# Recurrent block of a hybrid decoder trunk: where the high half of the gated product is rounded, when its last low half is formed, and the order of the last output projections

## The chip, the cores and the metric

The kernel runs on one core of a Trainium2 chip. The metric is device time in microseconds (us) of one execution; lower is better. The kernel computes a two-layer decoder trunk on 256 tokens of width 1024. All its large matrix products are done with split operands: each fp32 number is held as a high part (rounded to the matmul format fp32r) and a low part (the rest), and each product of two 128-row tiles is three matmuls, high x high, high x low and low x high.

## The reference, cut to what matters

```
h = x                                      # (1, 256, 1024)
for l in range(2):
    hn = rms_norm(h, mix_norm_g[l])
    mix = even_mixer(...) if l == 0 else odd_mixer(hn, ...)
    h = h + mix
    h = h + conv_ffn(rms_norm(h, ffn_norm_g[l]), ...)
return rms_norm(h, final_norm_g)

def odd_mixer(x, w_in, conv_w, conv_b, w_a, b_a, w_x, b_x, lam, w_out):
    gate_branch, xr = split(x @ w_in, 2)
    xr = causal_dwconv(xr, conv_w, conv_b)
    r, i = sigmoid(block_gemm(xr, w_a) + b_a), sigmoid(block_gemm(xr, w_x) + b_x)
    log_a = -8 * r * softplus(-lam)
    h = linear_scan(exp(log_a), sqrt(1 - exp(2 * log_a)) * i * xr)
    y = h * gelu(gate_branch)              # the gated product
    return y @ w_out                       # the output projection
```

The even mixer (attention and gated linear attention) also ends in a product with a 1024 x 1024 matrix, and the same helper computes it.

## The kernel before, in words

Everything is kept transposed: 128 channels on the partitions, 256 tokens along the free axis. A weight matrix comes in chunks of 128 x 1024 fp32 (512 KB). `load_w` keeps a short queue of chunks; `issue_w` starts the transfer of chunk i on SyncE, then forms its high part on ScalarE (`wh`, line 134) and its low part on VectorE (`wl`, line 135). Those two are called weight splits here. There are 204 chunks. Chunk 104 (`L1_C0`) is the first of layer 1's mixer; by the order in `L1_ORDER` its chunks 124 to 127 (`L1_C0 + 20` to `+ 23`) are the four chunks of the first half of the output projection ("o"), and 128 to 131 are the four of the second half ("h"); 132 is the first of the feed-forward network that follows.

The recurrent block handles channels in four pairs of 128-channel tiles, n = 0 to 3. For pair n, `recur` (line 690) makes the recurrence `hh[n]` with a scan on VectorE, and `finish` (line 697) makes the gated product. `finish` has one GeLU on ScalarE and three VectorE instructions on 128 x 512 elements: line 700 multiplies `hh` by `gb` straight into the rounded high part `Y[.., 0, :]`, line 701 makes the same product in fp32 in place, and line 702 subtracts the first from the second to give the low part `Y[.., 1, :]`. In the trace the tile `Y` is named `r`; the mixer result of layer 0 is named `m`.

`out_proj` (line 216) computes the output projection. Its eight 128 x 256 results m = 0 to 7 share four PSUM banks `acc[0]` to `acc[3]`, two to a bank (j = 0 and 1). `part(q, c)` adds k-tiles 2q and 2q+1 for four of the results; the four parts need only pairs 0 and 1 of the gated product, and each has 24 matmuls. `tail(n, fin)` then adds k-tiles 4 to 7 for the two results of bank n, again 24 matmuls, and calls `fin` for each result as soon as it is complete. K-tiles 4 and 5 come from pair 2, k-tiles 6 and 7 from pair 3. In `tail` all twelve matmuls of j = 0 come first, then `fin` of j = 0, then the twelve of j = 1. `fin` is `residual` (line 210): VectorE adds the result to the residual stream (line 211), ScalarE squares it for the next norm (line 172), VectorE accumulates the squares (line 179), and the two engines form the next product's input (lines 205 and 206).

The order of instructions on each engine is not the order of the program text: the framework schedules the whole program with a timing model of its own and then fixes one order for each engine. Engines then run their orders and wait for each other on semaphores. `order(first, then)` adds an edge that puts `then` behind `first` in that order, without a semaphore when both are on one engine. `state["hooks"]` holds such edges for weight splits: an entry under `("l", i)` puts the low weight split of chunk i on VectorE behind the given instruction. `passes` (line 141) issues the three matmuls for each k-tile in its list and returns them.

Of the kernel before, what the change touches and what calls it, by code (L numbers as in the profile page):

```python
# [8 lines left out]
F32 = mybir.dt.float32  # L9
# [3 lines left out]
AF = mybir.ActivationFunctionType  # L13
# [17 lines left out]
L1_C0 = 104  # L31
# [31 lines left out]
def trunk(ctx: ExitStack, tc: tile.TileContext, xT, w, wgk, wgk2, vec, cst, mskf, out):  # L63
    nc = tc.nc
# [7 lines left out]
    def bank(name, tag="g"):  # L72
        return pp.tile([P, 512], F32, tag=tag, bufs=BANKS[tag], name=name)

    def order(first, then):
        tc.add_manual_dep(then.ins, first.ins.name,
                          mybir.DependencyInfo(mybir.DependencyClass.NoSync, mybir.DependencyReason.DATA),
                          reason="issue order")
# [7 lines left out]
    def V(name, i):  # L86
        o = VOFF[name] + i
        return vt[:, o:o + 1]
# [25 lines left out]
    state = {"hooks": {}, "i": 0, "q": []}  # L114
# [3 lines left out]
    def load_w():  # L118
        while len(state["q"]) <= LOOK and state["i"] < NCH:
            state["q"].append(issue_w())  # L120
        return state["q"].pop(0)
# [19 lines left out]
    def passes(ps, ops, first=True, last=True, skip=False):  # L141
        n = len(ops)
        out = []
        for i, (ah, al, bh, bl) in enumerate(ops):
            for j, (a, b) in enumerate(((ah, bh), (ah, bl), (al, bh))):
                out.append(nc.tensor.matmul(ps, a, b, start=first and i + j == 0, stop=last and i == n - 1 and j == 2,  # L146
                                            skip_group_check=skip))
        return out

    def gemm(ps, wc, X, k0=0, first=True, last=True, nk=KT, skip=False):  # L150
        return passes(ps, [(wc[0][:, k * P:(k + 1) * P], wc[1][:, k * P:(k + 1) * P], X[:, k0 + k, 0, :], X[:, k0 + k, 1, :])
                    for k in range(nk)], first, last, skip)
# [8 lines left out]
    def new_m(name):  # L161
        return xp.tile([P, KT, 2, S], F32R, tag="m", name=name)
# [53 lines left out]
    def out_proj(M):  # L216
        acc = [bank(f"psout{i}", "g" if i < 3 else "l") for i in range(4)]
        opened = {}

        def part(q, c):  # L220
            wh, wl = load_w()
            for m in range(4 * c, 4 * c + 4):
                ps = acc[m // 2][:, (m % 2) * S:(m % 2 + 1) * S]
                ops = []
                for k in range(2):
                    o = k * 512 + (m % 4) * P
                    ops.append((wh[:, o:o + P], wl[:, o:o + P], M[:, 2 * q + k, 0, :], M[:, 2 * q + k, 1, :]))
                first = m not in opened
                mms = passes(ps, ops, first and m % 2 == 0, False, skip=True)
                if first:  # L230
                    opened[m] = mms[0]
                    if m % 2:
                        order(opened[m - 1], mms[0])

        def tail(n, fin):
            wh, wl = load_w()
            for j in range(2):
                ps = acc[n][:, j * S:(j + 1) * S]
                ops = []
                for k in range(4):  # L240
                    o = k * S + j * P
                    ops.append((wh[:, o:o + P], wl[:, o:o + P], M[:, 4 + k, 0, :], M[:, 4 + k, 1, :]))
                passes(ps, ops, False, True, skip=True)
                fin(ps, 2 * n + j)
        return part, tail

    def out_fin(X, gname, gi, norm):
        return lambda ps, m: residual(ps, m, X, gname, gi, norm)
# [29 lines left out]
    with tc.tile_pool(name="l0", bufs=1) as lp, tc.tile_pool(name="l0r", bufs=4) as lr:  # L278
# [106 lines left out]
        ps = bank("psbq")  # L385
# [9 lines left out]
        ps = bank("psbk")  # L395
# [81 lines left out]
        for nm in ("q", "k"):  # L477
            for m in range(2):
                ps = bank("psa")
# [56 lines left out]
        for pr in range(4):  # L536
            for j in range(2):
                PT[2 * pr + j] = softmax(2 * pr + j)
            ps = bank("pso", "t")
# [15 lines left out]
        for pr in range(4):  # L555
            ps = bank("pob", "l")
# [14 lines left out]
        for m in range(4):  # L571
            ps = bank("psog")
# [26 lines left out]
        fin = out_fin(X, "ffn_g", 0, norm)  # L599
# [40 lines left out]
    with tc.tile_pool(name="l1", bufs=1) as lp, tc.tile_pool(name="l1r", bufs=3) as lr:  # L640
        def pairs(name, dt=F32):
            return [lp.tile([P, 2, S], dt, name=f"{name}{n}") for n in range(4)]

        xc, rr, ii, aa, uu, tt, hh, gb = [pairs(n) for n in ("xc", "rr", "ii", "aa", "uu", "tt", "hh", "gb")]
        C1 = [lp.tile([P, 2, 2, S], F32R, name=f"c1{n}") for n in range(4)]
        Y = new_m("r")
        def xr_pair(n):
            ps = bank("psx")
            for j in range(2):
                gemm(ps[:, j * S:(j + 1) * S], load_w(), X)  # L650
            v = lr.tile([P, 2, S], F32, tag="v", name="v")
            nc.vector.tensor_mul(v, ps.rearrange("p (j t) -> p j t", j=2), rs[:, None, :].to_broadcast([P, 2, S]))
            for j in range(2):
                m = 2 * n + j
                nc.scalar.activation(xc[n][:, j, :], v[:, j, :], AF.Identity, bias=V("rc_b", m), scale=V("rc_w", 24 + m))
                for d in (1, 2, 3):
                    nc.vector.scalar_tensor_tensor(xc[n][:, j, d:], v[:, j, 0:S - d], V("rc_w", (3 - d) * 8 + m),
                                                   xc[n][:, j, d:], op0=ALU.mult, op1=ALU.add)
            split(C1[n][:, :, 0, :], C1[n][:, :, 1, :], xc[n])

        def gb_pair(n):
            ps = bank("psgb")
            for j in range(2):
                gemm(ps[:, j * S:(j + 1) * S], load_w(), X)
            nc.vector.tensor_mul(gb[n], ps.rearrange("p (j t) -> p j t", j=2), rs[:, None, :].to_broadcast([P, 2, S]))

        def gates(n):
            wh, wl = load_w()
            for gi, (dst, bn) in enumerate(((rr, "b_a"), (ii, "b_x"))):
                ps = bank("psgt", "s")  # L670
                for mt in range(2):
                    ops = []
                    for k in range(2):
                        o = gi * 512 + k * 256 + mt * 128
                        ops.append((wh[:, o:o + P], wl[:, o:o + P], C1[n][:, k, 0, :], C1[n][:, k, 1, :]))
                    passes(ps[:, mt * S:(mt + 1) * S], ops)
                for mt in range(2):
                    act(SIG, dst[n][:, mt, :], ps[:, mt * S:(mt + 1) * S], AF.Sigmoid,
                                         bias=V(bn, 2 * n + mt))
            nc.vector.tensor_mul(ii[n], ii[n], xc[n])  # L680

        def decay(n):
            for j in range(2):
                m = 2 * n + j
                nc.vector.tensor_scalar(rr[n][:, j, :], rr[n][:, j, :], cc[:, m:m + 1], None, op0=ALU.mult)
            for dst, f, sc in ((tt, AF.Tanh, 1.0), (uu, AF.Exp, 2.0), (aa, AF.Exp, 1.0)):
                act(EXP, dst[n], rr[n], f, scale=sc)
            nc.vector.scalar_tensor_tensor(tt[n], uu[n], 1.0, tt[n], op0=ALU.add, op1=ALU.mult)

        def recur(n):  # L690
            act(SQRT, tt[n], tt[n], AF.Sqrt, scale=-1.0)
            nc.vector.tensor_mul(uu[n], tt[n], ii[n])
            nc.gpsimd.memset(aa[n][:, :, 0:1], 0.0)
            fl = lambda t_: t_.rearrange("p a b -> p (a b)")
            nc.vector.tensor_tensor_scan(fl(hh[n]), fl(aa[n]), fl(uu[n]), 0.0, op0=ALU.mult, op1=ALU.add)

        def finish(n):
            s2 = slice(2 * n, 2 * n + 2)
            act(GELU, gb[n], gb[n], AF.Gelu_apprx_tanh)
            nc.vector.tensor_mul(Y[:, s2, 0, :], hh[n], gb[n])  # L700
            nc.vector.tensor_mul(hh[n], hh[n], gb[n])
            nc.vector.tensor_sub(Y[:, s2, 1, :], hh[n], Y[:, s2, 0, :].bitcast(F32))  # L702

        part = norm1 = None
        X1 = X
        for tok in L1_ORDER.split():
            if tok[0] == "o":
                if part is None:
                    part, tail = out_proj(Y)
                part(int(tok[1]), int(tok[2]))  # L710
            elif tok[0] == "h":
                if norm1 is None:
                    use(SQRT)
                    norm1 = Norm()
                    X1 = new_x()
                tail(int(tok[1]), out_fin(X1, "ffn_g", 1, norm1))
            else:
                {"x": xr_pair, "b": gb_pair, "g": gates, "e": decay, "s": recur, "f": finish}[tok[0]](int(tok[1:]))
# [112 lines left out]
```

## Time and profile before

| | |
|---|---|
| time, median of 3 runs | 649.29 us (645.31 to 649.8) |
| the profiled execution's own time | 646.74 us |
| its span | 645.0 us |
| TensorE matmuls busy | 630.7 us, 98% of the span |
| VectorE busy | 513.3 us, 80% |
| ScalarE busy | 406.0 us, 63% |
| mean granted TensorE clock | 0.993 of full speed |

The profile is one execution. Its span is the time from the first to the last instruction, and 1.74 us lie around it. Times in the rows are counted from the start of the span. In the timeline views each row is a run of like instructions on one engine: start, duration, engine, line, operation, output and inputs by name, count, and in square brackets the idle time before the first, with what ended it. A matmul's row is longer than the step to the next, because matmuls overlap.

### The profile page before, as it was taken

The numbers are of one execution on the slowest core, as the hardware profiler recorded it, in microseconds if no ns is written. First come the engines' busy times: TensorE is split into PE (matmuls) and PEld (weight loads), VectorE is DVE, ScalarE is ACT, GpSimd is POOL, SyncE is SP. The second block draws the span as 40 slices with busy tenths as digits, with TensorE's granted clock in tenths as the row PEclk, the third lists the DMA queues.
The fourth block names the chain that finished last, engine by engine and source line by source line (L and its number), as shares of the span: only waits on it lengthen the run. The fifth ranks groups of instructions, "written<-read, shape, count | busy, mean of one in ns | idle before, by whom it ended". The sixth has DMA issues, their size and how long they took to land.

```text
span 645.0 us, 12988 instructions
## 1 busy us (share of the span) xinstructions
PE 630.7 (98%) x5218; PEld 613.1 (95%) x5218; DVE 513.3 (80%) x902; ACT 406.0 (63%) x662; POOL 8.9 (1%) x36
## 2 busy tenths in 40 slices
PE   7999999999999999999999999989999999999995
PEld 4998888899999999999999999989999999999995
DVE  6699985467999999996577859996999999986532
ACT  7798454646776666675476578966666667674310
POOL 5000000000000000000000000000000000000000
PEclk8999999999999999999999999999999999999998
DMA  8823511534264485555277505544466545455201
GB/s 303 312 100 131 196 67 66 197 132 164 74 239 173 184 313 194 195 177 183 102 282 269 201 2 196 196 154 151 155 229 229 196 163 193 179 210 204 99 1 66
DMA packets 31516, 110.90 MB, mean 172 GB/s; under 512 B 3648, under 2 KB 4192, under 8 KB 31456
## 3 DMA queue, kind: packets, MB, share of 16 engines
q1 hardware_dynamic: 31456, 110.07, 47.5%
q8 instruction: 41, 0.67, 0.4%
q14 instruction: 19, 0.16, 0.1%
HBM read 109.01 MB, written 1.05 MB: 171 GB/s over the span
## 4 chain that ended last, share of the span: by engine, by line
PE 93%; DVE 2%; ACT 2%; issue 1%; DMA 1%; SPq 0%; DVEq 0%; ACTq 0%
PE psu L146 42%; PE psd L146 21%; PE psout L146 5%; PE psx L146 4%; PE psa L146 4%; PE pst L146 3%; PE psgb L146 3%; PE pl L465 2%; PE psog L146 2%; PE psgt L146 2%; PE psbq L146 1%; DVE wl L135 1%; PE psbk L146 1%; PE pss L514 1%; DMA big<-xT 1%
## 5 line engine op out<-in xcount | busy, mean ns | idle before, releaser
L134 ACT ACTIVATE wh<-w 128x1024 fp32r<-128x1024 f32 x204 | 212.5, 1056 | 112.8 <-PE psu L146 71.8
L135 DVE TENSOR_TENSOR wl<-w,wh 128x1024 fp32r<-128x1024 f32 x204 | 246.9, 1219 | 39.6 <-ACT wh L134 38.7
L146 PE MATMUL psu<-x,wh 128*128 128x256 f32 x1536 | 270.5, 280 | 0.0
L146 PEld LDWEIGHTS psu<-x,wh 128*128 128x128 f32 x1536 | 234.6, 189 | 0.0
L146 PE MATMUL psu<-x,wl 128*128 128x256 f32 x768 | 214.3, 280 | 0.0
L146 PEld LDWEIGHTS psu<-x,wl 128*128 128x128 f32 x768 | 144.7, 189 | 0.0
L146 PE MATMUL psd<-y,wh 128*128 128x256 f32 x768 | 134.6, 280 | 0.0
L146 PEld LDWEIGHTS psd<-y,wh 128*128 128x128 f32 x768 | 116.9, 188 | 0.0
L146 PE MATMUL psd<-y,wl 128*128 128x256 f32 x384 | 106.7, 279 | 0.0
L619 DVE SCALAR_TENSOR_TENSOR c<-v,big,c 128x255 f32<-128x255 f32 (+1 forms) x192 | 83.6, 475 | 0.0
L146 PEld LDWEIGHTS psd<-y,wl 128*128 128x128 f32 x384 | 72.1, 188 | 0.0
L617 ACT ACTIVATE c<-v,big 128x256 f32<-128x256 f32 x96 | 51.7, 589 | 0.6 <-DVE v L612 0.6
L172 ACT ACTIVATE sq<-big 128x256 f32<-128x256 f32 x40 | 15.4, 407 | 50.7 <-DVE big L211 50.6
L211 DVE TENSOR_TENSOR big<-big,psd 128x256 f32<-128x256 f32 x16 | 6.7, 420 | 35.3 <-PE psd L146 35.3
L612 DVE TENSOR_TENSOR v<-psu,rs 128x512 f32<-128x512 f32 x48 | 32.5, 681 | 0.0
L146 PE MATMUL psout<-r,wh 128*128 128x256 f32 x128 | 23.1, 282 | 2.0 <-DVE r L702 2.0
L146 PE MATMUL pst<-wh,x 128*128 128x256 f32 x128 | 24.2, 285 | 0.0
L146 PE MATMUL psout<-m,wh 128*128 128x256 f32 x128 | 23.7, 285 | 0.0
L146 PE MATMUL psx<-x,wh 128*128 128x256 f32 x128 | 23.0, 281 | 0.0
L146 PE MATMUL psgb<-x,wh 128*128 128x256 f32 x128 | 22.7, 280 | 0.0
L146 PE MATMUL psa<-x,wh 128*128 128x256 f32 x128 | 22.5, 280 | 0.0
L99 ACT ACT_TABLE_LOAD x17 | 21.8, 1283 | 1.0 <-PEq L823 0.7
(202 smaller groups left out, 850.5 us busy)
## 6 DMA issues: line engine op xcount, KB each, us to landing
w<-w SPq DMA_DIRECT2D x204, 512.0 KB, 4.3
big<-xT SPq DMA_DIRECT2D x4, 256.0 KB, 3.8
out<-o SPq DMA_DIRECT2D x4, 256.0 KB, 2.4
ct<-cst SPq DMA_DIRECT2D x1, 384.0 KB, 8.0
big<-vec SPq DMA_DIRECT2D x1, 224.0 KB, 7.9
mf<-mskf SPq DMA_DIRECT2D x1, 192.0 KB, 8.0
wg<-wgk SPq DMA_DIRECT2D x1, 64.0 KB, 2.0
big<-cst SPq DMA_DIRECT2D x1, 64.0 KB, 5.2
```

The source lines that it names most:

```text
L99: ld = nc.scalar.preload_act_table_set(name)
L134: hi = nc.scalar.activation(wh, wt, AF.Copy)
L135: lo = nc.vector.tensor_sub(wl, wt, wh.bitcast(F32))
L146: out.append(nc.tensor.matmul(ps, a, b, start=first and i + j == 0, stop=last and i == n - 1 and j == 2, skip_group_check=skip))
L172: ins = nc.scalar.activation(sq, t, AF.Square)
L211: nc.vector.tensor_add(h[:, m, :], h[:, m, :], ps)
L465: nc.tensor.matmul(pv[:, :, :, cs], Kb[li, I][:, ts_], qv[:, :, :, cs], start=True, stop=True)
L514: nc.tensor.matmul(ps[:, 128:384], q[r, P:S], k[r, 0:S], start=True, stop=False)
L612: nc.vector.tensor_mul(v, ps.rearrange("p (j t) -> p j t", j=2), rs[:, None, :].to_broadcast([P, 2, S]))
L617: nc.scalar.activation(c[:, j, :], v[:, j, :], AF.Identity, bias=V("fc_b", layer * 48 + ch), scale=wv(2))
L619: nc.vector.scalar_tensor_tensor(c[:, j, d:], v[:, j, 0:S - d], wv(2 - d), c[:, j, d:], op0=ALU.mult, op1=ALU.add)
```

## The change

In `finish`, the high part is no longer a second multiplication on VectorE. The fp32 product is formed first (VectorE), ScalarE copies it with rounding into the high part, and VectorE then subtracts as before. The low part of the last pair, n = 3, is put ahead of the low weight split of chunk `L1_C0 + 25` (129, the second chunk of the second half of the projection). In `tail`, the 24 matmuls go by pairs of k-tiles: k-tiles 4 and 5 for j = 0, the same for j = 1, then k-tiles 6 and 7 for j = 0, then for j = 1, and these 24 are kept in that order. `tail` is called by both layers, `finish` by layer 1 alone.

```
         def tail(n, fin):
             wh, wl = load_w()
-            for j in range(2):
+            mms = []
+            for kp, j in ((0, 0), (0, 1), (1, 0), (1, 1)):
                 ps = acc[n][:, j * S:(j + 1) * S]
                 ops = []
-                for k in range(4):
+                for k in (2 * kp, 2 * kp + 1):
                     o = k * S + j * P
                     ops.append((wh[:, o:o + P], wl[:, o:o + P], M[:, 4 + k, 0, :], M[:, 4 + k, 1, :]))
-                passes(ps, ops, False, True, skip=True)
-                fin(ps, 2 * n + j)
+                mms += passes(ps, ops, False, kp == 1, skip=True)
+                if kp:
+                    fin(ps, 2 * n + j)
+            for a_, b_ in zip(mms, mms[1:]):
+                order(a_, b_)
         return part, tail
...
         def finish(n):
             s2 = slice(2 * n, 2 * n + 2)
             act(GELU, gb[n], gb[n], AF.Gelu_apprx_tanh)
-            nc.vector.tensor_mul(Y[:, s2, 0, :], hh[n], gb[n])
             nc.vector.tensor_mul(hh[n], hh[n], gb[n])
-            nc.vector.tensor_sub(Y[:, s2, 1, :], hh[n], Y[:, s2, 0, :].bitcast(F32))
+            nc.scalar.activation(Y[:, s2, 0, :], hh[n], AF.Copy)
+            lo = nc.vector.tensor_sub(Y[:, s2, 1, :], hh[n], Y[:, s2, 0, :].bitcast(F32))
+            if n == 3:
+                state["hooks"].setdefault(("l", L1_C0 + 25), []).append(lo)
```

## Rows read from the trace of the kernel before

**Rows 1.** The page, busy time by engine: us (share), instructions.
```profile
PE 630.7 (98%) x5218; PEld 613.1 (95%) x5218; DVE 513.3 (80%) x902; ACT 406.0 (63%) x662; POOL 8.9 (1%) x36
```

**Rows 2.** The longest wait of TensorE's matmuls, whole span: us in total, times, longest.
```profile
PE psout L146 <- DVE r L702: 2.0, 2, 1.5
```

**Rows 3.** Timeline of TensorE around the second half of layer 1's output projection.
```profile
418.59 0.63 PE L146 MATMUL psout<-r,wh 128*128 128x256 f32 x4
419.68 0.38 PE L146 MATMUL psout<-r,wh 128*128 128x256 f32 x1 [0.47 <-DVE r L702]
...
422.48 0.27 PE L146 MATMUL psout<-r,wh 128*128 128x256 f32 x1
424.29 0.39 PE L146 MATMUL psout<-r,wh 128*128 128x256 f32 x1 [1.54 <-DVE r L702]
...
432.41 0.40 PE L146 MATMUL psu<-x,wh 128*128 128x256 f32 x2
```

**Rows 4.** Projection matmuls (psout) by stretch: length; PE, PEld, DVE busy (count); clock, DMA.
```profile
419.60:424.00 4.40, 3.07 (x24) 2.87 (x24) 0.00 (x0) 1.00 0.38 133
424.00:434.00 10.00, 8.28 (x68) 8.07 (x68) 3.34 (x8) 1.00 0.44 153
```

**Rows 5.** Timeline of VectorE in layer 1's block, to the residual adds.
```profile
406.53 0.68 DVE L702 TENSOR_TENSOR r<-hh,r 128x512 fp32r<-128x512 f32 x1
...
411.43 1.23 DVE L135 TENSOR_TENSOR wl<-w,wh 128x1024 fp32r<-128x1024 f32 x1 [0.67 <-ACT wh L134]
...
416.02 0.68 DVE L700 TENSOR_TENSOR r<-hh,gb 128x512 fp32r<-128x512 f32 x1
416.63 1.22 DVE L695 TENSOR_TENSOR_SCAN hh<-aa,uu 128x512 f32<-128x512 f32 x1
417.76 0.67 DVE L701 TENSOR_TENSOR hh<-hh,gb 128x512 f32<-128x512 f32 x1
...
418.95 0.68 DVE L702 TENSOR_TENSOR r<-hh,r 128x512 fp32r<-128x512 f32 x1
419.55 1.21 DVE L135 TENSOR_TENSOR wl<-w,wh 128x1024 fp32r<-128x1024 f32 x1
...
421.29 2.35 DVE L135 TENSOR_TENSOR wl<-w,wh 128x1024 fp32r<-128x1024 f32 x2
423.56 0.68 DVE L702 TENSOR_TENSOR r<-hh,r 128x512 fp32r<-128x512 f32 x1
425.19 0.42 DVE L211 TENSOR_TENSOR big<-big,psout 128x256 f32<-128x256 f32 x1 [0.95 <-PE psout L146]
...
427.10 0.41 DVE L211 TENSOR_TENSOR big<-big,psout 128x256 f32<-128x256 f32 x1
...
430.51 0.42 DVE L179 TENSOR_TENSOR ssq<-sq 128x256 f32<-128x256 f32 x1
```

**Rows 6.** Timeline of ScalarE in the same block.
```profile
391.52 0.62 ACT L155 ACTIVATE c<-xc 128x512 fp32r<-128x512 f32 x1
...
415.87 1.28 ACT L99 ACT_TABLE_LOAD   x1
417.16 2.96 ACT L134 ACTIVATE wh<-w 128x1024 fp32r<-128x1024 f32 x3
425.64 0.42 ACT L172 ACTIVATE sq<-big 128x256 f32<-128x256 f32 x1 [5.52 <-DVE big L211]
```

**Rows 7.** Low weight splits (line 135) in stretches: VectorE busy us (count), granted clock, DMA.
```profile
0.00:386.00 386.00, 145.30 (x120) 1.00 0.50 178
386.00:419.20 33.20, 13.32 (x11) 1.00 0.56 191
419.20:425.00 5.80, 3.56 (x3) 1.00 0.45 157
```

**Rows 8.** The chain that ended last, layer 0's second projection half: start, length, what.
```profile
136.39 1.41 PE psout L146 x12
...
139.80 8.49 PE psout L146 x72
```

## The prediction

> **What bounds the kernel now.** I read the page's busy times first. TensorE's matmuls fill 98% of the span [rows 1], so a saving must take idle time out of TensorE; work taken off VectorE (80%) or ScalarE (63%) counts only where TensorE waits for it. So the next view is TensorE's waits. The longest entry of the whole span is 2.0 us in two waits, for line 702, the low part of the gated product [rows 2]. This is the place that the change works on. The timeline shows both waits in the second half of layer 1's projection [rows 3]: four matmuls from 418.59, then nothing until 419.68; matmuls until 422.48, then nothing until 424.29. Matmuls follow each other every 0.117 us (24 from 419.68 to 422.48, 2.80 us). The missing time by starts is 419.68 - (418.59 + 4 x 0.117) = 0.62 us and 424.29 - (422.48 + 0.117) = 1.69 us, together 2.3 us. It reads 2.0 in the waits because a matmul's row is longer than its step. So 2.3 us, 0.36% of the time, is the most that this place can give. The granted clock is 1.00 there, the 2.4 GHz level, before and after the waits [rows 4], so no clock is to be won.
>
> Why is the low part late? VectorE's timeline [rows 5] has line 702 for pair 2 at 418.95 and for pair 3 only at 423.56, though the scan of pair 3 ends at 417.85. Between them lie line 701 of pair 3 and three weight splits, one at 419.55 and two at 421.29, some 1.14 us each from start to start: 3.4 us. These splits are not urgent. Of the low splits, 120 + 11 lie ahead of 419.2 [rows 7]; in index order those are chunks 0 to 130, so the three are 131, 132 and 133: the last quarter of the projection and two chunks of the next stage.
>
> How TensorE's 96 matmuls were ordered also matters. It did 4 + 24 = 28, then waited, then 68 [rows 3, 4]. 28 is 4 x 7: in each of four sums, six for k-tiles 4 and 5 and the first for k-tile 6, which needs only the high part; the next one needs the late low part. The four sums are the first halves (j = 0) of the four banks, I think: if they were the two halves of two banks, m = 0 and 1 would be among the first four adds (425.19 to 427.10), and their squares could be summed soon; the first such sum comes at 430.51 [rows 5]. So a bank's second half seems to start only when the add of its first half has read it.
>
> **The change part by part.** (1) The high part moves from VectorE to ScalarE. VectorE loses four instructions, 0.60 us each from start to start (416.02 to 416.63): 2.4 us in all, of which the two for pairs 2 and 3 lie in the late stretch, 1.2 us. ScalarE gains four rounding copies; the nearest row is the same kind of copy of the same shape, 0.62 us [rows 6]. For pairs 0 and 1 I cost this at nothing. The four parts start at 418.59 - 96 x 0.117 = 407.4, and the two that need pair 1 at 413.0; its low part ended at 407.2 [rows 5], so 5.8 us of TensorE work cover it. A copy that lands in ScalarE's chain of activations ahead of the last scan can delay it by 0.5, and the moved weight split (below) gives VectorE more than that back.
>
> For pairs 2 and 3 the copy adds a crossing between engines to the path. I keep the scan of pair 2 where it was. Line 701 of pair 2 takes the slot at 416.02, the scan of pair 3 ends at 417.85, and its line 701 at 418.43. ScalarE is in a table load until 417.16 and then did three weight splits until 420.12; after that it stood idle 5.52 us [rows 6]. Copy 2 can run from 417.16 to 417.8, so low part 2 from 418.4 to 419.0. Copy 3 runs at 418.5 if ScalarE is free, or after one 1.0 us split at 418.8, and ends at 419.1 to 419.4; low part 3 ends at 419.8 to 420.1, against 424.24.
>
> VectorE runs its queue in order, so the wait for copy 3 also holds the splits and adds behind it, by at most one copy, 0.6 us. With the copies ahead of the three splits, the last of these ends 1.2 us later than now, in ScalarE's idle 5.5 us.
>
> (2) Low part 3 goes ahead of the split of chunk 129. By the count of splits that one ran at 411.43 [rows 5, 7], so it moves past the whole end of the recurrence: 1.14 us are freed there, and the splits of 129, perhaps 130, 131 and the next two now follow low part 3: 129 ends at about 421.2, and each later one 1.14 us behind. TensorE comes to bank 1 after one whole bank, 24 x 0.117 = 2.8 us after 418.6, so at 421.4; then a chunk each 2.8 us. It just holds. Nothing moves on SyncE by itself, but its next transfer waits for these splits; chunks 132 and 133, split 9 us ahead of their use, are the cover.
>
> (3) The tail order. The first twelve matmuls of a bank, 1.4 us, need only pair 2. As the other banks' splits come behind low part 3, it is due at 420.0; in the order of before, with 28 matmuls ahead, it was due at 421.9 and came at 424.24. TensorE loses 0.4 waiting for low part 2 at 419.0 plus signalling, and 0 to 0.4 for low part 3. I take 0.6 of loss in all (ends 0 and 1.3, the higher with a copy and a split in the way), so 2.3 - 0.6 = 1.7 us are won.
>
> The order also applies in layer 0. There TensorE did 12 matmuls, then 12, then 72 without a wait [rows 8]. The 12 (three for k-tile 4 in each bank) are still to be had in the new order, one bank's first half each, and after k-tile 5 another 36. So nothing is lost; the bounds are 0 and the nearest wait, 0.5.
>
> One rule speaks against the new order. By the rows above, TensorE leaves a bank's second half alone until the add of the first half has read it. The Trainium skill (PSUM — Partial Sum Buffer, PSUM bank collisions raise a hardware error) says the same: two engines must be kept apart by bank, not by address. The order of the adds here agrees, the first sum of squares coming at 430.51 only. What this would cost is the third rival.
>
> **What is late next.** If the tail ends 1.7 us earlier, the next stage starts at 430.7, with its first two chunks split by 425. After that TensorE is bound by its own work (98%), so the gain stays until the end.
>
> **The rivals.** *A, most of the stall goes.* The sum gives 645.0 - 1.7 = 643.3 of span and 645.0 for the profiled execution of 646.74. The four times of this program (645.31, 646.74, 649.29, 649.8) lie 4.5 us apart, more than the gain. I put the sum on their median, 648.0: 646.3 us, or 1.7 below whichever of them the run falls on.
>
> *B, the copies come too late.* Lines 701 end at 416.7 and 418.4. If ScalarE's order keeps its three splits together from 417.16 to 420.12, copy 2 ends at 420.7, copy 3 at 421.25, and the low parts at 421.4 and 422.0. TensorE then loses 421.5 - 418.7 = 2.8 instead of 2.3: 0.5 slower, 648.5. For it speaks that VectorE's order put three splits ahead of a low part now; against it, that the products are ready sooner than the end of the table load or of the first split.
>
> *C, the other side: the add stands between the quarters of a bank.* Now a bank's second half comes after the other three first halves, so its add is long done. In the new order only six matmuls of the other half, which come ahead of the first half's last six, are left to fill; the last six of j = 1 must wait until the add has read j = 0. If TensorE's order goes bank by bank, each of eight banks pays at least the rest of a matmul (0.16) and an add (0.42), 0.6 us; with a split of 1.14 in front on VectorE, 1.7. That is 4.8 us at the lower price, less 1.7: 3.1 slower, 651.1; with a split at every bank some 9 more, 660. It decides at three banks: if the wait is filled at six of the eight, it costs 1.2 and the gain stands. Against it: the present order already mixes four banks, and that is open to the new one, since the fixed order holds within a bank only; and the next stage's input and first chunk of the next stage can fill the last bank.
>
> **How the numbers follow.** A 0.58 (own range 643.0 to 648.4), B 0.22, C 0.17, something else 0.03. The predicted time is A's, 646.3. The low end is the fastest time shown less the whole stall, 645.31 - 2.3 = 643.0. The high end takes in B and C's lower price on the median, 651. One per cent, 6.5 us, is about what a measurement of this kernel can tell from no change. No idle of that size is there to win, so faster by over 1% has 0.03, from the scatter of the times; slower by over 1% needs C at its higher price, 0.04; within 1% is 0.93.
>
> **What would show it.** Right: line 702 for pair 3 ends near 420, TensorE's waits for it fall under 1 us, the next stage's first matmul comes 1 to 2 us earlier against the end of the parts, and layer 0's second half still runs without a wait. B shows as line 702 waiting for the rounding copy with three splits in front on ScalarE; C as TensorE waiting for line 211, in both layers. The sum is wrong if the new schedule rearranges the stages around, which the trace of before can't show.

## The result, and the profile after

The changed kernel takes 652.87 us in the median of 12 runs (648.57 to 654.16), the kernel before 648.82 in 13 runs beside them (645.31 to 649.8). The ratio is 1.0069, with a 95% interval of 1.0043 to 1.0094: slower. One more run of the changed kernel, of 884.6 us at a mean granted clock of 0.652, is left out. The forecast of 646.3 us, and its range up to 651.0, were wrong, and so was its sign.

The profiled execution took 650.23 us with a span of 648.4, at a mean granted clock of 0.992, against 646.74, 645.0 and 0.993: 3.4 us more span. Each of the two traces holds one drop of the clock outside its last 10 us, and both drops cost about 1.7 us: 0.68 and 0.98 in the two 5 us slices from 10 to 20 us before, 0.93 and 0.72 in those from 115 to 125 after. So the 3.4 us are not the clock's. At a mean clock of 0.996 the changed kernel took 648.57 us, and the kernel before 645.29 in the runs beside the first experiments: 3.3 us apart. So the traces hold the loss; the medians differ by 0.7 us more, which is small beside the scatter that goes with the clock in either kernel (from 648.57 us at 0.996 to 654.16 at 0.986 in the changed one; for the other see the last section).

The page's first part, busy time by engine, of the changed kernel:

```profile
PE 632.7 (98%) x5218; PEld 613.4 (95%) x5218; DVE 511.2 (79%) x898; ACT 409.2 (63%) x666; POOL 8.9 (1%) x36
```

Against [rows 1], VectorE has four instructions and 2.1 us less, ScalarE four more and 3.2 us more, as the change says. The span did not follow VectorE.

**Where the 3.4 us are.** The start of a stage is read from the tile views: the first time of a matmul row of its PSUM tile. `psout` is the output projection (from `m` in layer 0, from `r` in layer 1) and `psd` the down-projection of the feed-forward network behind it. In the changed kernel:

```profile
L146 PE MATMUL psout<-m,wh x6: 280/280/281, 123.0 to 123.8; 128*128 128x256 f32 x6
...
L146 PE MATMUL psd<-y,wh x10: 278/279/280, 286.4 to 287.9; 128*128 128x256 f32 x10
...
L146 PE MATMUL psout<-r,wh x9: 280/280/288, 410.5 to 411.9; 128*128 128x256 f32 x9
...
L146 PE MATMUL psd<-y,wh x20: 278/280/281, 571.6 to 574.9; 128*128 128x256 f32 x20
```

and in the kernel before:

```profile
L146 PE MATMUL psout<-m,wh x7: 278/280/281, 122.8 to 123.8; 128*128 128x256 f32 x7
...
L146 PE MATMUL psd<-y,wh x28: 277/278/281, 283.2 to 287.9; 128*128 128x256 f32 x28
...
L146 PE MATMUL psout<-r,wh x27: 278/281/287, 407.3 to 411.9; 128*128 128x256 f32 x27
...
L146 PE MATMUL psd<-y,wh x38: 278/279/282, 568.4 to 574.9; 128*128 128x256 f32 x38
```

So from layer 0's projection to its down-projection it is 163.4 us against 160.4, **3.0 us more**; from there to layer 1's projection 124.1 in both; from layer 1's projection to its down-projection 161.1 in both. The rest is 0.2 before and 0.2 behind. Layer 0, costed at nothing, lost all of it; layer 1, costed at 1.7 us won, won nothing.

**Layer 0.** TensorE's longest waits between 136 and 165 us of the changed kernel (us in total, times, longest); before, this stretch has none:

```profile
PE psu L146 <- ACT wh L134: 0.7, 1, 0.7
PE psu L146 <- DVE wl L135: 0.6, 1, 0.6
PE psu L146 <- DVE x L206: 0.5, 1, 0.5
```

None is in the projection. All three are in `psu`, the first product of the next stage, and TensorE's timeline shows where:

```profile
148.32 0.28 PE L146 MATMUL psout<-m,wl 128*128 128x256 f32 x1
148.44 0.40 PE L146 MATMUL psu<-x,wh 128*128 128x256 f32 x2
...
149.81 0.39 PE L146 MATMUL psu<-x,wl 128*128 128x256 f32 x1 [0.62 <-DVE wl L135]
...
151.42 0.51 PE L146 MATMUL psu<-x,wh 128*128 128x256 f32 x2 [0.74 <-ACT wh L134]
152.41 0.39 PE L146 MATMUL psu<-x,wh 128*128 128x256 f32 x1 [0.48 <-DVE x L206]
```

The projection itself is as long as before: `psu` starts 148.44 - 123.0 = 25.4 us after it, and before 148.1 - 122.8 = 25.3. But ten `psu` matmuls need 152.41 - 148.44 = 3.97 us instead of 10 x 0.117: 2.8 us lost. (The three waits read 1.8 us in sum, because a matmul's row is longer than its step; by starts they are 0.8, 1.0 and 0.8.) VectorE's and ScalarE's timelines show why; first those of the changed kernel:

```profile
145.03 1.42 DVE L211 TENSOR_TENSOR big<-big,psout 128x256 f32<-128x256 f32 x4 [2.05 <-PE psout L146]
...
146.75 0.42 DVE L211 TENSOR_TENSOR big<-big,psout 128x256 f32<-128x256 f32 x1
...
148.53 1.22 DVE L135 TENSOR_TENSOR wl<-w,wh 128x1024 fp32r<-128x1024 f32 x1
```

```profile
145.48 0.42 ACT L172 ACTIVATE sq<-big 128x256 f32<-128x256 f32 x1 [2.97 <-DVE big L211]
...
147.01 1.05 ACT L134 ACTIVATE wh<-w 128x1024 fp32r<-128x1024 f32 x1
```

and of the kernel before:

```profile
141.94 1.41 DVE L211 TENSOR_TENSOR big<-big,psout 128x256 f32<-128x256 f32 x4 [0.78 <-PE psout L146]
...
144.13 0.42 DVE L211 TENSOR_TENSOR big<-big,psout 128x256 f32<-128x256 f32 x1
...
145.87 1.22 DVE L135 TENSOR_TENSOR wl<-w,wh 128x1024 fp32r<-128x1024 f32 x1
```

```profile
142.40 0.42 ACT L172 ACTIVATE sq<-big 128x256 f32<-128x256 f32 x1 [1.69 <-DVE big L211]
...
144.32 1.05 ACT L134 ACTIVATE wh<-w 128x1024 fp32r<-128x1024 f32 x1
```

The first four sums are added (line 211) from 145.03 instead of 141.94. The fifth add, the first of a second half, marks the end of a bank's tail and so of its weight chunk: 146.75 instead of 144.13. The next weight split on each engine moves by the same step, ScalarE's from 144.32 to 147.01, VectorE's from 145.87 to 148.53. Ahead of the first add ScalarE stands idle for 2.97 us and VectorE for 2.05 (1.69 and 0.78 before). The first add now leads the next stage by 3.4 us (148.44 - 145.03), before by 6.2.

**Layer 1.** The lines of `finish` are 704 (fp32 product), 705 (ScalarE's copy) and 706 (low part) in the changed kernel. Its timelines of VectorE, ScalarE and TensorE, in the place of [rows 3, 5, 6]:

```profile
419.01 1.27 DVE L704 TENSOR_TENSOR hh<-hh,gb 128x512 f32<-128x512 f32 x2
422.94 1.29 DVE L706 TENSOR_TENSOR r<-hh,r 128x512 fp32r<-128x512 f32 x2 [2.66 <-ACT r L705]
424.15 4.62 DVE L135 TENSOR_TENSOR wl<-w,wh 128x1024 fp32r<-128x1024 f32 x4
```

```profile
419.09 1.28 ACT L99 ACT_TABLE_LOAD   x1
420.38 2.01 ACT L134 ACTIVATE wh<-w 128x1024 fp32r<-128x1024 f32 x2
422.29 1.14 ACT L705 ACTIVATE r<-hh 128x512 fp32r<-128x512 f32 x2
```

```profile
421.73 0.28 PE L146 MATMUL psout<-r,wl 128*128 128x256 f32 x1
422.96 1.11 PE L146 MATMUL psout<-r,wh 128*128 128x256 f32 x5 [0.95 <-ACT r L705]
...
434.66 0.27 PE L146 MATMUL psu<-x,wh 128*128 128x256 f32 x1
435.17 0.39 PE L146 MATMUL psu<-x,wh 128*128 128x256 f32 x1 [0.24 <-DVE x L206]
...
437.39 0.40 PE L146 MATMUL psu<-x,wh 128*128 128x256 f32 x2
438.44 0.39 PE L146 MATMUL psu<-x,wl 128*128 128x256 f32 x1 [0.66 <-DVE wl L135]
```

The product of the last pair is ready at 420.28, before the table load ends (420.37), and both copies come only at 422.29, behind two weight splits: ScalarE's order had them there. VectorE waits 2.66 us for them with four splits in its queue. TensorE's wait in the projection falls to one of 0.95 us; 0.24 and 0.66 us come back at the start of the next stage. By starts the three gaps are 1.1, 0.4 and 0.8 us, the 2.3 us of before.

### The profile page after: what moved, and what is told of

Its sections match the earlier page's. It is cut to its first block, busy times and chain, and to the rows that moved or that the text cites. A ratio compares the mean times of both kernels' runs of the same rounds, so it can differ in the third digit from the quotient of the medians.

```text
span 648.4 us, 13000 instructions
## 1 busy us (share of the span) xinstructions
PE 632.7 (98%) x5218; PEld 613.4 (95%) x5218; DVE 511.2 (79%) x898; ACT 409.2 (63%) x666; POOL 8.9 (1%) x36
## 4 chain that ended last, share of the span: by engine, by line
PE 90%; ACT 4%; DVE 3%; issue 1%; DMA 1%; SPq 0%; DVEq 0%; ACTq 0%
PE psu L146 41%; PE psd L146 21%; PE psx L146 3%; PE psa L146 3%; PE pst L146 3%; PE psout L146 3%; PE psgb L146 3%; PE psog L146 2%; PE pl L469 2%; DVE wl L135 2%; PE psgt L146 2%; ACT wh L134 1%; PE psbk L146 1%; PE psbq L146 1%; ACT L99 1%
```

## The experiments

After the result two theories stood for each layer.
- Layer 0: *chunks held*: the pair order uses the weight chunks of all four banks to the end, so the buffers for the next stage's splits come free late. *Results late*: the adds, squares and inputs behind the sums are late by themselves, whatever the buffers. A third candidate was the fixed order of 24 matmuls (the edges) rather than the pair order.
- Layer 1: *copies behind splits* (rival B): it is ScalarE's queue order that eats the gain. Against it: the pair order of the tail eats it.

All runs, with the kernel before beside each group (medians 647.57, 647.66 and 648.84 us for the first four, the next four and the last four). Columns b and d are the two stages read as above in the profiled execution: layer 0's projection to its down-projection, and the same in layer 1; before they are 160.4 and 161.1.

| run | median us (runs) | ratio to before, 95% | b | d |
|---|---|---|---|---|
| changed kernel | 652.87 (12) | 1.0069, 1.0043 to 1.0094 | 163.4 | 161.1 |
| e1_pairs_layer0 | 650.96 (9) | 1.0048, 1.0023 to 1.0073 | 163.4 | 160.7 |
| e2_layer1_alone | 647.78 (10) | 1.0006, 0.9983 to 1.0029 | 160.5 | 163.6 (clock) |
| e3_finish_alone | 648.07 (10) | 0.9995, 0.997 to 1.0019 | 160.4 | 161.0 |
| e4_own_slots_layer0 | 648.39 (10) | 1.0002, 0.998 to 1.0024 | 161.0 | 162.4 (clock) |
| e5_copy_first | 645.59 (10) | 0.9954, 0.993 to 0.9978 | 160.5 | 158.7 |
| e6_copy_first_own_slots | 646.54 (10) | 0.9985, 0.9963 to 1.0007 | 160.5 | 159.4 |
| e7_pairs_layer0_free | 651.13 (10) | 1.0053, 1.0038 to 1.0069 | 164.8 (clock) | 160.7 |
| e8_before_own_slots | 649.9 (10) | 1.0039, 1.0017 to 1.0061 | 161.0 | 162.2 |
| e9_copy_first_old_tail | 644.08 (4) | 0.9939, 0.9917 to 0.9961 | 160.4 | 158.6 |
| e10_low_first_alone | 644.05 (4) | 0.9939, 0.9919 to 0.9958 | 160.4 | 159.4 |
| e11_low_first_pairs | 647.46 (10) | 0.9987, 0.9965 to 1.0009 | 160.4 | 160.5 |
| e12_pairs_layer1 | 648.75 (10) | 1.0013, 0.9987 to 1.0038 | 160.4 | 162.9 (clock) |

"Clock" marks a stage in which the granted clock fell in that execution; each of e2, e4, e7 and e12 lost about 1.7 us to it there (read as in the last section, from the clock of two 5 us slices). Between traces whose code for the stage is the same, d differs by up to 0.4 us (160.7 in e1 and e7 against 161.1 before), and once by 0.8 (e2, 163.6 - 1.7 = 161.9, against the changed kernel's 161.1), and e8, whose buffers alone are changed, has 1.1 more; a difference of d below 0.8 us is not read as an effect.

### Which part costs: e1, e2, e3

`out_proj` gets a switch, so that each layer's tail can have either order.

```
-    def out_proj(M):
+    def out_proj(M, by_pairs):
...
-        return part, tail
+        return part, tail_k if by_pairs else tail_j    # pair order, order of before
```

**e1**: the kernel before, with the pair order in layer 0 alone.

> The kernel before, with the k-tile pair order in layer 0's tail alone; layer 1's tail and finish are those of before. Theory L0 (the loss of 3.4 us between the two profiles sits in layer 0: the first residual add comes at 145.03 instead of 141.94 and the next stage's first matmuls wait for weight splits and input): the span is 2.5 to 3.3 us longer than that of before, the matmuls of the next stage stand still for about 2 to 3 us after 148, and layer 1 is unchanged with its two waits of 2.0 us. Rival (the change of the order costs nothing in layer 0 and the longer time is scatter or a clock dip): span within 0.7 us of before.

**e2**: the changed kernel, with the order of before in layer 0.

> The changed kernel, with layer 0's tail in the order of before; finish and layer 1's tail as changed. Theory L0: the 2.9 us of layer 0 come back, the span is 645.0 to 645.8 and the ratio to before 0.998 to 1.002, because layer 1 alone gains a shorter wait (2.3 to 1.1 us by starts) and gives about as much back at the start of its feed-forward network. Rival (layer 1 is where the time is lost): span stays above 647.5.

**e3**: the kernel before with the changed `finish` alone (copy on ScalarE and the edge for the last low part), both tails as before.

> The kernel before, with the changed finish alone (high part by ScalarE, last low part ahead of the split of chunk 129); both tails in the order of before. If the rounding copies stand behind two weight splits on ScalarE as in the changed kernel (copies at 422.3 there, products ready at 420.2), VectorE waits 2 to 3 us for the copy and the low parts end near 420.5 to 421 on the clock of before: TensorE's waits at the second half of the projection stay 1 to 2 us, span 644.3 to 645.5. If the order of the tail caused the late copies, the low part of pair 3 ends by 420.1 as predicted and the span is 643.0 to 643.8.

e1 has the whole 3.0 us of layer 0 (163.4, with waits of 0.8, 0.7 and 0.5 us for the same three), and is slower, 1.0048. e2 is within 0.3% of the kernel before. The two ratios add to 1.0054, inside the interval of the changed kernel: the parts make the whole, and layer 0's tail order is the loss. e3 shows that layer 1's `finish` gains nothing by itself either. Its copies stand behind two splits as in the changed kernel (splits 418.58 to 420.59, copies from 420.49), VectorE waits 2.65 us, TensorE 0.93 us in the projection and 0.7 us for the next stage's input.

### Layer 0, the order or the edges: e7

e1 without the edges between the matmuls:

```
-            for a_, b_ in zip(mms, mms[1:]):
-                order(a_, b_)
```

> As e1 (pair order in layer 0 alone), without the edges that keep the 24 matmuls in order. Theory: the program order by pairs alone makes the scheduler finish the second pairs last, so the loss of 3.0 us between the start of the projection and the next stage's second half stays within 0.7 us. Rival (the edges are the cost): the loss falls under 1 us.

The waits are the same (0.8, 0.6, 0.5 us), b is 164.8 with some 1.7 us of lowered clock in it, so 163.1 without, and the time is 1.0053. The edges cost nothing that can be measured; the order in which the text issues the work does.

### Layer 0, chunks held or results late: e4, e8

The splits of each chunk take one of six buffers in turn, so chunk 34 reuses that of chunk 28, the first of layer 0's four tail chunks. e4 gives chunks 28 to 31 buffers of their own, in the changed kernel; e8 does the same in the kernel before, as the control.

```
-        pre = "p" if L1_C0 <= i < L1_C0 + NPRE else ""
-        nb = NPRE if pre else 6
+        pre = "p" if L1_C0 <= i < L1_C0 + NPRE else "q" if 28 <= i < 32 else ""
+        nb = {"p": NPRE, "q": 4, "": 6}[pre]
```

> The changed kernel, with high and low tiles of their own for the four weight chunks of layer 0's tail (28 to 31), so that the six shared slots are free for the next stage's chunks while the tail runs. Theory slots (chunk 34's split at 147.01 waits for the slot of chunk 28, which the pair order holds until the last quarter): the splits of chunks 34 to 36 run before the first residual add at 145, and the waits at the start of the next stage fall from 2.9 us to under 1: span 645.8 to 646.5. Rival late results (the adds, squares and input splits of eight results are squeezed into the last 3.4 us, whatever the slots): some of the waits stay, for the input tile rather than the weights, 1 to 2 us: span 646.5 to 648.

> The kernel before, with tiles of their own for the four weight chunks of layer 0's tail: the control to e4. If the slots are a limit only under the pair order, the stretch from the start of layer 0's projection to the down-projection stays at 160.4 us within 0.3 us and the ratio to before is 0.998 to 1.002. If own slots are worth 2.4 us in any order, it falls to about 158 us and the time by 0.4%.

Low weight splits ahead of the first add in e4 (length; VectorE busy us and count; granted clock, DMA share and GB/s), and the add itself on VectorE's timeline:

```profile
0.00:142.70 142.70, 46.17 (x38) 0.99 0.49 170
```

```profile
142.78 1.08 DVE L211 TENSOR_TENSOR big<-big,psout 128x256 f32<-128x256 f32 x3 [2.77 <-PE psout L146]
```

In the changed kernel the same stretch has 34:

```profile
0.00:145.00 145.00, 41.41 (x34) 0.99 0.46 167
```

Before it is 34 too: chunks 0 to 33, and chunk 34 must wait for chunk 28's buffer. In e4 the first add is as late as in the changed kernel (142.78 - 120.8 = 22.0 us after the projection's start; there 145.03 - 123.0 = 22.0), so the results are as late, but four more chunks are split beforehand, and TensorE has no wait at all between 136 and 165 us. b is 161.0, and the control with the old order has 161.0 as well. With buffers free the pair order costs nothing in this stage: *results late* alone is ruled out, *chunks held* stands. It is no remedy. The control met neither outcome that was expected of it: it is slower than the kernel before by 0.39% (0.17 to 0.61). Its trace reaches layer 0's projection 1.9 us earlier (120.9), and then loses 0.6 us in b, 0.7 between the two stages and 1.1 in d (162.2). Why stays open.

### Layer 1, the copies' place: e5, e6, e9

e5 is e2 (pair order in layer 1 alone) with the copies of pairs 2 and 3 put ahead of ScalarE's high split of chunk 130:

```
-            nc.scalar.activation(Y[:, s2, 0, :], hh[n], AF.Copy)
+            up = nc.scalar.activation(Y[:, s2, 0, :], hh[n], AF.Copy)
+            if n in (2, 3):
+                state["hooks"].setdefault(("h", L1_C0 + 26), []).append(up)
```

e6 is e5 with own buffers for chunks 128 to 131, the copies ahead of the splits of 130, 131 and 132. e9 is e5 with the order of before in both layers' tails.

> As e2 (layer 0's tail in the order of before), and the two last rounding copies put ahead of ScalarE's high split of chunk 130. Theory late copies (VectorE waited 2.7 us for copies that stood behind two weight splits): the copies run straight after the table load, VectorE's wait for them falls from 2.7 to under 1 us, the low part of pair 3 ends within 1.5 us of its product, and TensorE's wait at the start of the second half (1.1 us by starts) goes. The start of the next stage still waits about 1 to 2 us for the input and a split: span 1.0 us shorter than e2 without its clock dip, 643.0 to 644.6. Rival (the wait only moves to the splits behind the low parts): TensorE's waits in the second half stay about 1 us in sum, span as e3, 644.3 to 645.5 without a dip.

> As e5, with high and low tiles of their own for chunks 128 to 131 as well, and the copies ahead of chunks 130 to 132 on ScalarE. Theory slots: in layer 1 too the pair order holds the tail's four weight slots until its last quarter; with own slots the waits for input or splits at the start of the next stage fall under 0.7 us and the span to 642.3 to 643.5 without a dip, 2 us below before. Rival late results: the waits at the start of the next stage stay at 1 to 2 us.

> As e5, with the tail of layer 1 in the order of before too (so no tail is changed; finish is, with the two last copies ahead of chunk 130's high split). The stretch from the start of layer 1's projection to the next down-projection was 161.1 us before and 158.7 in e5. If the pair order of layer 1 matters (the work that needs only pair 2 covers the low part of pair 3), this one is 159.5 to 160.5. If the gain of e5 is that of the earlier low parts alone, it is 158.5 to 159.2.

e9's ScalarE and VectorE timelines (lines 700, 701 and 704 are its product, copy and low part):

```profile
415.34 1.28 ACT L99 ACT_TABLE_LOAD   x1
416.63 1.16 ACT L701 ACTIVATE r<-hh 128x512 fp32r<-128x512 f32 x2
417.69 2.94 ACT L134 ACTIVATE wh<-w 128x1024 fp32r<-128x1024 f32 x3
```

```profile
415.82 1.27 DVE L700 TENSOR_TENSOR hh<-hh,gb 128x512 f32<-128x512 f32 x2
417.30 1.29 DVE L704 TENSOR_TENSOR r<-hh,r 128x512 fp32r<-128x512 f32 x2 [0.21 <-ACT r L701]
418.51 2.35 DVE L135 TENSOR_TENSOR wl<-w,wh 128x1024 fp32r<-128x1024 f32 x2
```

The copies now run right behind the table load, VectorE waits 0.21 us instead of 2.66, and TensorE has no wait from 400 to 450 us. d is 158.6 (e5: 158.7), 2.5 us less than before: the whole stall of 2.3 us. Against e3 (161.0), e9 differs only by the place of the two copies: that is rival B's mechanism shown by its removal. The tail order makes no difference to d here (158.7 against 158.6). e5 did better than expected: TensorE waited 0.2 us at the next stage where 1 to 2 were forecast. Own buffers (e6) added nothing (159.4).

### Layer 1, the edge without the copy: e10, e11, e12

e10 is the kernel before with the one edge: the low part of pair 3 goes ahead of the low split of chunk 129. The high part stays on VectorE. e11 adds the pair order in layer 1's tail; e12 is the kernel before with that order alone.

```
-            nc.vector.tensor_sub(Y[:, s2, 1, :], hh[n], Y[:, s2, 0, :].bitcast(F32))
+            lo = nc.vector.tensor_sub(Y[:, s2, 1, :], hh[n], Y[:, s2, 0, :].bitcast(F32))
+            if n == 3:
+                state["hooks"].setdefault(("l", L1_C0 + 25), []).append(lo)
```

> The kernel before, with nothing but the last low part put ahead of the low split of chunk 129; high parts stay on VectorE. VectorE then does six instructions for pairs 2 and 3 in a row, 3.6 us, with no split between and no wait for ScalarE. Theory: the low part of pair 3 ends 3 to 4 us earlier against the end of the parts, TensorE's waits at the second half fall from 2.3 to under 1 us by starts, and the stretch is 159.0 to 160.0. Rival (the ScalarE copy is what makes it early): 160.5 to 161.3.

> As e10, with the pair order in layer 1's tail alone. If the pair order hides what is left of the low part's lateness, the stretch is 0.3 to 0.8 us shorter than e10; if its late results cost as in layer 0, it is equal or longer.

> The kernel before, with the pair order in layer 1's tail alone and the old finish. The pair order makes 48 matmuls free of pair 3 instead of 28, 2.3 us more of cover, and chunks 129 and 130 are split early here: the wait for the low part of pair 3 (1.7 us by starts) goes. Theory slots: what is won comes back as waits for splits or input at the start of the next stage, as in layer 0: stretch 160.5 to 162.0. Rival (no such cost in layer 1): 159.0 to 159.8.

e10's VectorE timeline, in the place of [rows 5], and its only wait of TensorE from 400 to 450 us:

```profile
416.09 1.27 DVE L700 TENSOR_TENSOR r<-hh,gb 128x512 fp32r<-128x512 f32 x2
417.27 1.29 DVE L701 TENSOR_TENSOR hh<-hh,gb 128x512 f32<-128x512 f32 x2
418.48 1.29 DVE L702 TENSOR_TENSOR r<-hh,r 128x512 fp32r<-128x512 f32 x2
419.68 4.63 DVE L135 TENSOR_TENSOR wl<-w,wh 128x1024 fp32r<-128x1024 f32 x4
```

```profile
PE psu L146 <- DVE x L206: 0.7, 1, 0.7
```

The low part of pair 3 ends at 419.77 instead of 424.24, and d falls by 1.7 us, to 159.4. The pair order on top takes 1.1 us of it back (e11, 160.5), in waits of 1.1 and 0.6 us for the next stage's input and first chunk. Alone (e12) it shortens the wait for the low part to 0.5 us but waits 0.9 and 0.8 us at the next stage; its 162.9 less the 1.7 us of clock is 161.2, against 161.1 before. In layer 1 the pair order never won.

e9 and e10 beat both kernels: 0.9939 of the kernel before, some 4.0 us (their medians lie 4.8 us below). By their traces 2.5 and 1.7 us of that are the edit's. Their fastest runs, 643.26 and 643.66 us at mean clocks of 0.995 and 0.997, stand 1.8 and 1.4 us below the fastest of the kernel before in that group (645.03 at 0.996). The rest goes with the clock of four runs each and is not shown to come from the edit. Nor do these runs tell e9 from e10.

## Why the prediction was wrong

**What bounds the kernel: right.** Three unurgent splits stood ahead of the last low part, and TensorE's stall of 2.3 us came from that. e10 changes nothing but this order and wins 1.7 us; e9 wins 2.5. That the time would stay within one per cent held too.

**The step that failed: part (3), layer 0, "So nothing is lost; the bounds are 0 and the nearest wait, 0.5".** It asked whether TensorE finds work inside the projection. It does: 25.4 us against 25.3. But the step did not ask when the projection hands things on. With the pair order no sum is complete before the last third of the tail, and no weight chunk before its last quarter: the first add leads the next stage by 3.4 us instead of 6.2, the fifth add moves from 144.13 to 146.75, and with it the split into the first freed buffer, from 144.32 to 147.01. The price was 3.0 us, nearly all of it in three waits (0.6, 0.7 and 0.5 us; 2.6 by starts) in the stage behind; e4 takes the waits away with buffers alone. It was not among the three cases: A and B priced layer 0 at nothing, and C looked for the cost inside the bank. The trace of before and the code had what was needed to see it: 34 low splits ahead of the first add, six buffers, and the next splits right behind the first add of a second half.

**The second step that failed: part (1), the time of copy 3, on which the term of -1.7 us in layer 1 rests.** The term was 0.0. The sum let copy 3 run "at 418.5 if ScalarE is free, or after one 1.0 us split at 418.8", and priced VectorE's wait at 0.6 us at most. Measured: copies at 422.29, behind two splits, and a wait of 2.66 us. This is rival B's mechanism, which had 0.22, with three splits for two; its effect of +0.5 us came out as 0, since the wait in the projection fell to 0.95 us while 0.9 us more came at the next stage. The prediction wrote that "for it speaks that VectorE's order put three splits ahead of a low part now". That row should have weighed more than the argument set against it, that the products are ready before the table load ends: they were (420.28 against 420.37), and the two splits still went first. The edge bound the low part, on VectorE, but nothing bound the copy that it waits for, on ScalarE.

**The size of the moved work: right.** Two copies took 1.14 us together (0.53 each by starts, from e9's rows) against 0.62 for one in the sum, and VectorE lost 2.1 us against 2.4.

**Rival C: refuted, though its time (651.1) was the nearest.** TensorE never waits for line 211 in the changed kernel. The Trainium skill (PSUM — Partial Sum Buffer, PSUM bank collisions raise a hardware error) wants two engines kept apart by bank, not by address. No run here shows whether they were, as the rows don't name the bank. They don't speak against it: in layer 0 the four first halves' adds run from 145.03 to 146.45 as a group, while TensorE's `psout` rows go on to 148.32. No wait of TensorE was the price of it.

**The sum.** Predicted -1.7; measured +3.0 in layer 0, 0.0 in layer 1, 0.4 in the rest: +3.4 of span. What brought the 0.7 us by which the medians differ beyond that is not settled.

## What to carry to other kernels

An accumulation order that keeps the matmul engine just as busy can still cost time, by when it completes its first results and gives back its operands' buffers: after the stage itself, read the first instructions of the next one and count the buffers they wait for. A priority given to an instruction must be given to each of its producers on other engines as well; otherwise the in-order queue behind it waits with it. Where a queue's order is the trouble, try the one edge that mends it before moving work to another engine: here it alone gave 1.7 us, the copy without an edge of its own took them back (e3), and with one it gave 2.5 (e9).

## What the runs showed of the hardware

The kernel before, unchanged, scatters with TensorE's mean granted clock. Of 30 runs beside the first group the fastest took 645.29 us at 0.996 and the slowest 650.29 at 0.987; the correlation of time and clock is -0.97. The traces show stretches of some 4 us in which the clock drops, in some executions and not in others. In e7 one follows the waits of the next stage (length; TensorE, weight load, VectorE, ScalarE, GpSimd busy and count; granted clock, DMA share, GB/s):

```profile
145.00:150.00 5.00, 5.00 (x44) 4.98 (x43) 3.61 (x11) 3.15 (x7) 0.00 (x0) 1.00 0.00 0
150.00:155.00 5.00, 3.13 (x15) 2.36 (x14) 5.00 (x8) 5.00 (x10) 0.00 (x0) 0.84 0.48 161
155.00:160.00 5.00, 5.00 (x38) 5.00 (x37) 4.23 (x10) 2.34 (x6) 0.00 (x0) 0.82 0.73 252
160.00:165.00 5.00, 5.00 (x45) 5.00 (x44) 1.63 (x3) 2.19 (x3) 0.00 (x0) 1.00 0.34 116
```

By these rows (0.16 + 0.18) x 5 = 1.7 us are lost. In slices of 1 us the clock is below 1.00 only from 153 to 157 us (0.70, 0.50, 0.50, 0.60): that is the 1.2 GHz level, with 2.4 GHz on either side. TensorE's matmuls had been busy for only 3.13 us of the 5 us slice in which it fell. e2 (0.87 and 0.79 from 430 to 440) and e12 (0.82 and 0.84 from 435 to 445) show the same behind their waits in layer 1. But the changed kernel and e1, with the same waits as e7 in layer 0, have 1.00 there; and the changed kernel's clock dropped from 119 to 123 us and e7's from 81 to 86 with no wait of TensorE in the 10 us before. So such waits are neither enough nor needed for a drop; what decides it was not tried.
